# Squares of the attention output: made once a head by GpSimd and VectorE instead of tile by tile by ScalarE

## The chip, the cores and the metric

The kernel runs on one core of a Trainium2 chip. The metric is the device time of one execution in microseconds (us). The engines are TensorE (PE in the profile; PEld is its weight load), VectorE (DVE), ScalarE (ACT), GpSimd (POOL) and SyncE (SP), which issues most of the DMA transfers. SBUF is the on-chip memory of 128 partitions; PSUM is the memory into which TensorE writes its results.

## The reference, cut to what matters

Two layers of a mixer run over 512 latent and 256 context tokens. Each layer has one input projection, an RWKV-7 part, a short convolution, differential attention with 4 heads of width 128, and one output projection. The change is in the attention:

```python
def diff_attend(q, k, v, lam, scale):
    s = jnp.einsum('bqhjd,bkhjd->bhjqk', q, k).astype(jnp.float32) * scale
    p = jax.nn.softmax(s, axis=-1)
    attn = p[:, :, 0] - lam * p[:, :, 1]
    return jnp.einsum('bhqk,bkhe->bqhe', attn.astype(v.dtype), v)
...
    def finish(o, z):
        o = rms_norm(o, subln_g) * (1.0 - lam_init)
        return o.reshape(o.shape[0], o.shape[1], D_ATTN) * jax.nn.silu(z)
```

`rms_norm` divides each row of 128 outputs of a head by the root of the mean of its squares. Those sums of squares are what the change makes in another way. Layer 0 needs the outputs of all 768 tokens (6 tiles of 128 rows a head), layer 1 those of the 512 latent tokens (4 tiles).

## The kernel before, in words

The attention stage of a layer goes through the heads one by one, and through a head in units. A unit is one tile of 128 query rows, or the two context tiles together. Layer 0 has 5 units a head (`ORD`, the context unit second), layer 1 has 4. The loop at L1329 is a software pipeline written by hand: at step x, TensorE makes the scores (`sc`) of unit x+3, VectorE finds their negated row maxima (`mx`), ScalarE makes the exponentials (`e`) of unit x+2 with their sums (`oden`), VectorE makes a coefficient (`cf`) and combines the two softmaxes of unit x+1 (`e<-e,cf,e`; GpSimd does the last 256 columns, L1233 and L1234), and for unit x TensorE transposes the result (`aTp`), ScalarE copies it to SBUF (`aT`, L1257) and TensorE multiplies it with the values (`av`).

`drain` follows one unit later. ScalarE copies each 128x128 output tile of `av` from PSUM to the head's tile `O` (L1276) and runs a Square over the same PSUM tile whose accumulator gives the sum of squares in a column of `ss` (L1279, written to a scratch tile `osq`; the profile calls `ss` `oss`).

`finish` works on a whole head after its last unit, in two parts. The first part, begun one unit into the next head (`FI` = 1), loads the head's gate `zT` by a DMA from SP's queue, turns the sums into scales `ors` (a chain of some 12 small operations on VectorE: `oss`, `rs_i`, `rs_y`, `rs_t`, `ors`), and lets GpSimd scale `O` (L1297; VectorE for the last head). The second part stands behind the `av` of the next head's unit 3 (`FI2` = 3): TensorE transposes `O` (`oT`), VectorE multiplies by the gate (`zT<-oT,zT`), ScalarE casts the result (L1310) and GpSimd makes the rest to it (L1311). This place, where the finished head meets the pipeline of the next, is called a joint below; a layer has three, as the last head is finished after the stage. The place where a head's last `O` tile has been copied and the next head goes on is called a boundary.

What sets the order: TensorE's instructions keep the order of the program throughout the stage (`AL` = 1), so a transpose `oT` that waits holds up the `aTp` and the scores behind it. On VectorE and ScalarE the instructions of the unit pipeline (`dv`, `ac`) keep their order among themselves; what `finish` issues is put among them by a scheduler when the kernel is built. The PSUM tiles `aTp`, `av` and `oT` share two buffers (tag "a"). `zT` has one buffer (`ZB` = 1), so the `zT` of a head is free when L1311 of the head before has read it.

Of the kernel before, what the change touches and what calls it, by code (L numbers as in the profile page):

```python
# [10 lines left out]
F32 = mybir.dt.float32  # L11
# [3 lines left out]
ALU = mybir.AluOpType  # L15
AX = mybir.AxisListType
PSUM = bass.MemoryType.PSUM

P = 128
# [87 lines left out]
def build(tc, A):  # L107
    nc = tc.nc
    ctx = ExitStack()
    S, G = nc.scalar, nc.gpsimd  # L110
# [14 lines left out]
    V = Vec()  # L125
# [63 lines left out]
    def small(n, tag, pool=None, bufs=2):  # L189
        return (pool or sm).tile([P, n], F32, tag=tag, bufs=bufs, name=tag)  # L190
# [5 lines left out]
    for l in range(L):  # L196
        t = cst.tile([P, NCC], F32, name=f"chan{l}")
# [962 lines left out]
    def attention(l, lat, cx, pool, az_done, hd0):  # L1160
        last = l == L - 1
        li = 0.8 - 0.6 * math.exp(-0.3 * l)
        n = NL if last else NT
# [7 lines left out]
        ntt = 4 if last else 6  # L1171
        vA = pool.tile([P, 6, 512], F32, name="vA")
        ss = small(24, "oss", pool, 1)
# [11 lines left out]
        def dv(i):  # L1185
            order("v", i)

        def ac(i):
            order("s", i)
# [81 lines left out]
        def drain(u):  # L1271
            for po, tt in zip(u["po"], u["tt"]):
                if AC & 4:
                    dv(V.tensor_copy(Os[u["h"]][:, tt], po))
                else:
                    ac(S.copy(Os[u["h"]][:, tt], po))  # L1276
                osq = pool.tile([P, P], F32, tag="osq", bufs=2, name="osq")
                col = u["h"] * 6 + tt
                ac(S.activation(osq, po, AF.Square, accum_out=ss[:, col:col + 1]))  # L1279

# [1 line left out]

        def finish(h, O):
            zT = pool.tile([P, NT], F32, tag="zT", bufs=ZB, name="zT")
            nc.sync.dma_start(out=zT[:, :n], in_=zd[l][h, :, :n])
            E1 = V if h == 3 else G
            c0 = h * 6
# [3 lines left out]
            for _ in range(2):  # L1291
# [6 lines left out]
                             in1=rs[:, :ntt].unsqueeze(2).to_broadcast([P, ntt, P]), op=ALU.mult)  # L1298
# [27 lines left out]
        def at(i):  # L1326
            return us[i] if 0 <= i < len(us) else None

        for x in range(-3, len(us)):  # L1329
            u, p, c, e, w = at(x), at(x - 1), at(x + 1), at(x + 2), at(x + 3)  # L1330
# [9 lines left out]
            if p:  # L1340
                drain(p)
# [27 lines left out]
            if u and u["i"] == FI and u["h"]:  # L1369
                fins.append(finish(u["h"] - 1, Os[u["h"] - 1]))  # L1370
                next(fins[-1])
            if u and u["i"] == FI2 and u["h"]:
                next(fins[-1])
        drain(us[-1])
        fin = finish(3, Os[3])
        next(fin)
        return fin
# [75 lines left out]
    for l in range(L):  # L1453
        F.update(FL[l])
        last = l == L - 1
        n = NL if last else NT
# [248 lines left out]
```

## Time and profile before

| what | value |
|---|---|
| median of three runs | 1156.28 us (1147.5 to 1362.1) |
| the profiled execution | 1150.33 us, span 1148.3 us, mean granted clock 0.973 |
| busy share of the span | PE 90%, DVE 64%, ACT 46%, POOL 42% |
| chain that ended last, by engine | PE 36%, DVE 24%, ACT 6%, issue 6%, POOL 4%, DMA 3% |
| the gate's load into `zT`, issue to landing | 3.0 us (384 KB, layer 0), 3.1 us (256 KB, layer 1) |
| attention of layer 0, of layer 1 | some 481 to 572 us, 1008 to 1092 us of the span |

The span is the time from the profile's first instruction to its last; the execution's own time is 2.0 us longer. Shares of the whole span mix stages with different limits, so the change has to be read in the two attention stages alone.

### The profile page before, as it was taken

How to read it: one execution, taken by the hardware profiler on the slowest of the kernel's cores; microseconds unless marked ns; L12 is line 12 of the kernel's file. 1: busy time of each engine (PE TensorE's matmuls, PEld its weight loads, DVE VectorE, ACT ScalarE, POOL GpSimd, SP SyncE). 2: the span in 40 equal slices, each digit the busy share in tenths (PEclk: the TensorE clock that was granted, in tenths of full speed). 3: DMA queues.
4: the chain of work that ended last, by engine and by line, in shares of the span. 5: the costliest groups of instructions: out<-in, count | busy, mean ns of one | idle time of the engine just before them, and what ended most of it. 6: DMA issues, size and time to landing. Idle time of an engine off the chain costs nothing.

```text
span 1148.3 us, 25449 instructions
## 1 busy us (share of the span) xinstructions
PE 1034.9 (90%) x9850; PEld 847.2 (74%) x9850; DVE 731.3 (64%) x1712; ACT 523.7 (46%) x1330; POOL 488.0 (42%) x508
## 2 busy tenths in 40 slices
PE   4899989999798999989899899998987999888897
PEld 1577968777687877878787786866766897777775
DVE  3530658687666253499847857676986824579944
ACT  4332462452362232378723564654343533338731
POOL 1311534434625422464522346254474454456632
PEclk9899999999899999999999999999998999999999
DMA  9573322212423365754052452232232345555143
GB/s 350 182 245 121 89 73 57 61 31 87 141 73 112 121 189 175 223 165 108 15 188 74 147 167 88 71 100 78 72 97 85 92 132 150 165 158 170 47 156 110
DMA packets 92088, 142.55 MB, mean 124 GB/s; under 512 B 28192, under 2 KB 36416, under 8 KB 91968
## 3 DMA queue, kind: packets, MB, share of 16 engines
q1 hardware_dynamic: 88512, 136.14, 38.4%
q10 hardware_dynamic: 3456, 4.80, 1.3%
q8 instruction: 77, 1.26, 0.5%
q14 instruction: 43, 0.35, 0.1%
HBM read 110.99 MB, written 25.71 MB: 119 GB/s over the span
## 4 chain that ended last, share of the span: by engine, by line
PE 36%; DVE 24%; ACT 6%; issue 6%; POOL 4%; DMA 3%; SPq 1%; DVEq 0%; ACTq 0%; POOLq 0%
PE pcl L134 10%; PE op L134 6%; PE ptl L134 4%; DVE mx L118 4%; PE pcc L134 2%; PE ptc L134 2%; PE ch L132 2%; DVE e L118 2%; DVE bk L118 2%; DVE rs_t L118 1%; DMA mraw<-in_mod_w_dram 1%; DVE qkr L118 1%; POOL wlo L261 1%; PE av L134 1%; PE yps L132 1%
## 5 line engine op out<-in xcount | busy, mean ns | idle before, releaser
L261 POOL TENSOR_TENSOR wlo<-wraw,whi 128x512 fp32r<-128x512 f32 x134 | 181.9, 1360 | 312.2 <-ACT whi L258 279.4
L134 PE MATMUL pcl<-lat,whi 128*128 128x512 f32 (+1 forms) x928 | 295.3, 395 | 1.0 <-POOL lat L344 0.8
L134 PEld LDWEIGHTS pcl<-lat,whi 128*128 128x128 f32 x928 | 170.2, 190 | 40.2 <-issue 6.4
L134 PE MATMUL pcl<-lat,wlo 128*128 128x512 f32 (+1 forms) x464 | 185.1, 399 | 5.1 <-POOL wlo L261 3.7
L258 ACT CAST whi<-wraw 128x512 fp32r<-128x512 f32 x144 | 88.4, 618 | 159.8 <-DMA wraw<-in_w_in_dram 38.5
L134 PE MATMUL pcc<-ctx,whi 128*128 128x256 f32 x576 | 112.8, 292 | 2.0 <-DVE ctx L118 1.7
L134 PEld LDWEIGHTS pcl<-lat,wlo 128*128 128x128 f32 x464 | 88.0, 190 | 28.2 <-POOL wlo L261 5.6
L134 PEld LDWEIGHTS pcc<-ctx,whi 128*128 128x128 f32 x576 | 95.2, 197 | 9.0 <-issue 3.2
L134 PE MATMUL pcc<-ctx,wlo 128*128 128x256 f32 x288 | 84.4, 293 | 2.0 <-DVE wlo L118 2.0
L134 PE MATMUL ptl<-whi,lat 128*128 128x256 f32 x384 | 82.0, 299 | 1.1 <-ACT qkr L1090 1.1
L1222 ACT ACTIVATE e<-sc,mx 128x768 f32<-128x768 f32 (+1 forms) x80 | 66.5, 834 | 19.5 <-DVE mx L118 14.0
L118 DVE TENSOR_REDUCE mx<-sc 128x1 f32<-128x768 f32 (+1 forms) x72 | 63.7, 918 | 14.0 <-PE sc L134 14.0
L134 PE MATMUL av<-vA,aT 128*128 128x128 f32 x416 | 59.6, 287 | 14.0 <-ACT aT L1257 13.8
L134 PEld LDWEIGHTS av<-vA,aT 128*128 128x128 f32 x416 | 54.2, 195 | 20.9 <-ACT aT L1257 17.9
L134 PEld LDWEIGHTS ptl<-whi,lat 128*128 128x128 f32 x384 | 65.4, 201 | 3.4 <-ACT qkr L1090 1.4
L118 DVE TENSOR_TENSOR R<-s,cs 128x384 f32<-128x384 f32 (+1 forms) x96 | 47.0, 529 | 20.9 <-PE s L132 20.2
L134 PEld LDWEIGHTS pcc<-ctx,wlo 128*128 128x128 f32 x288 | 56.7, 197 | 4.6 <-DVE wlo L118 2.2
L134 PE MATMUL ptl<-wlo,lat 128*128 128x256 f32 x192 | 57.6, 300 | 0.0
L920 POOL TENSOR_TENSOR pz<-zu,pc 64x128 f32<-64x128 f32 x88 | 37.4, 425 | 45.9 <-DVE zu L118 41.1
L134 PE MATMUL sc<-KH,QS 128*128 128x256 f32 (+1 forms) x144 | 51.4, 371 | 4.7 <-ACT e L1222 2.9
L134 PE MATMUL sc<-KL,QS 128*128 128x256 f32 (+1 forms) x144 | 45.0, 334 | 0.0
L1233 POOL TENSOR_TENSOR e<-e,cf 128x256 f32<-128x256 f32 x32 | 26.3, 823 | 42.0 <-DVE cf L118 13.9
(449 smaller groups left out, 2450.6 us busy)
## 6 DMA issues: line engine op xcount, KB each, us to landing
wraw<-in_w_in_dram SPq DMA_DIRECT2D x144, 256.0 KB, 2.7
mraw<-in_mod_w_dram SPq DMA_DIRECT2D x96, 256.0 KB, 4.6
KH<-qd SPq DMA_DIRECT2D x32, 192.0 KB, 4.1
oraw<-in_w_out_dram SPq DMA_DIRECT2D x20, 256.0 KB, 3.7
qd<-qks SPq DMA_DIRECT2D x12, 384.0 KB, 2.4
qd<-qkr SPq DMA_DIRECT2D x12, 384.0 KB, 2.5
qks<-qkr SPq DMA_DIRECT2D x64, 64.0 KB, 2.1
zu<-vd SPq DMA_DIRECT2D x96, 32.0 KB, 2.2
```

The lines of the kernel that those rows point to most:

```text
L118: i = f(*a, **k)
L132: tc.keep_in_program_order(nc.tensor.matmul(*a, **k))
L134: i = nc.tensor.matmul(*a, **k)
L258: S.copy(hi, raw)
L261: eng.tensor_tensor(out=lo, in0=raw, in1=hi.bitcast(F32), op=ALU.subtract)
L920: G.tensor_tensor(out=pz[d][hr], in0=zu[d][hr, :, h, :], in1=prepd[d][1][hr, :, cc[d][1]].unsqueeze(2).to_broadcast([64, 2, HD]), op=ALU.mult)
L1222: ac(S.activation(ej[:, c], pb[:, c], AF.Exp, bias=mx[:, i:i + 1], accum_out=den[:, u["h"] * 6 + tt, j:j + 1]))
L1233: G.tensor_tensor(out=e1, in0=e1, in1=cf[:, 0:1].to_broadcast([P, NC]), op=ALU.mult)
```

## The change

For the first three heads of each layer `drain` only copies `O`. The sums of squares of such a head are made in `finish`: GpSimd multiplies the whole `O` tile by itself (128x768 in layer 0, 128x512 in layer 1) into the head's `zT` tile, VectorE sums each 128 columns into the head's columns of `ss`, and the load of the gate into `zT` follows. Head 3 keeps its Squares on ScalarE. `osq` has one buffer instead of two. In the changed file the square is at L1289, the reduction at L1290, the load at L1291, and the lines from the old L1285 on stand 6 further (L1297 becomes L1303, L1311 becomes L1317).

```diff
--- before.py
+++ after.py
@@ -1274,7 +1274,9 @@
                     dv(V.tensor_copy(Os[u["h"]][:, tt], po))
                 else:
                     ac(S.copy(Os[u["h"]][:, tt], po))
-                osq = pool.tile([P, P], F32, tag="osq", bufs=2, name="osq")
+                if u["h"] < 3:
+                    continue
+                osq = pool.tile([P, P], F32, tag="osq", bufs=1, name="osq")
                 col = u["h"] * 6 + tt
                 ac(S.activation(osq, po, AF.Square, accum_out=ss[:, col:col + 1]))
 
@@ -1282,6 +1284,10 @@
 
         def finish(h, O):
             zT = pool.tile([P, NT], F32, tag="zT", bufs=ZB, name="zT")
+            if h < 3:
+                sq = zT[:, :n].rearrange("p (t c) -> p t c", c=P)
+                G.tensor_tensor(out=sq, in0=O[:, :ntt], in1=O[:, :ntt], op=ALU.mult)
+                V.tensor_reduce(out=ss[:, h * 6:h * 6 + ntt], in_=sq, axis=AX.X, op=ALU.add)
             nc.sync.dma_start(out=zT[:, :n], in_=zd[l][h, :, :n])
             E1 = V if h == 3 else G
             c0 = h * 6
```

TensorE's order is the same in both kernels. On VectorE and GpSimd the order changes at every boundary and joint of the two stages.

At the boundary behind the second head of layer 0, VectorE's instructions stand in this order before (`oss`, `rs_i`, `rs_y`, `rs_t` are the finished head's chain, the rest is the unit pipeline):

```order
L118 RECIPROCAL cf<-oden 128x2
L118 SCALAR_TENSOR_TENSOR cf<-cf,lm_579,oden 128x2
L118 TENSOR_TENSOR oss<-oss,r_6473 128x6
L118 SCALAR_TENSOR_TENSOR e_6363<-e_6377,cf,e_6363 128x256 x2
L118 TENSOR_TENSOR oss<-oss,r_6473 128x6
L118 TENSOR_SCALAR oss<-oss 128x6
L118 TENSOR_SCALAR rs_i<-oss 128x6
L118 TENSOR_SCALAR rs_y<-rs_i 128x6
L118 TENSOR_TENSOR rs_t<-rs_y 128x6
L118 TENSOR_REDUCE mx<-sc 128x1 x2
```

The run of small operations ahead of `mx` is what moves in the next fence, which shows the same place in the changed kernel:

```order
L118 SCALAR_TENSOR_TENSOR cf<-cf,lm_579,oden 128x2
L118 SCALAR_TENSOR_TENSOR e_6343<-e_6357,cf,e_6343 128x256 x2
L118 TENSOR_REDUCE oss<-zT 128x6
L118 TENSOR_REDUCE mx<-sc 128x1 x2
L118 RECIPROCAL cf<-oden 128x1
L118 TENSOR_TENSOR oss<-oss,r_6451 128x6
```

The reduction now stands ahead of `mx`, and the chain behind it is spread over the units that follow.

At the first joint of layer 0, GpSimd's instructions stand in this order before:

```order
L1297 TENSOR_TENSOR O<-O,ors 128x768
L1233 TENSOR_TENSOR e_6256<-e_6256,cf 128x256
L1234 TENSOR_TENSOR e_6243<-e_6243,e_6256 128x256
L1233 TENSOR_TENSOR e_6318<-e_6318,cf 128x256
L1234 TENSOR_TENSOR e_6285<-e_6285,e_6318 128x256
L1311 TENSOR_TENSOR lat_113<-zT,lat_112 128x512
L1311 TENSOR_TENSOR ctx_115<-zT,ctx_114 128x256
```

The scaling of `O` stands two units' products ahead of L1311 there. In the changed kernel the same place reads:

```order
L1233 TENSOR_TENSOR e_6240<-e_6240,cf 128x256
L1234 TENSOR_TENSOR e_6227<-e_6227,e_6240 128x256
L1233 TENSOR_TENSOR e_6300<-e_6300,cf 128x256
L1303 TENSOR_TENSOR O<-O,ors 128x768
L1234 TENSOR_TENSOR e_6267<-e_6267,e_6300 128x256
L1317 TENSOR_TENSOR lat_113<-zT,lat_112 128x512
L1317 TENSOR_TENSOR ctx_115<-zT,ctx_114 128x256
L1289 TENSOR_TENSOR zT<-O 128x768
```

The scaling has moved back behind the `e<-e,cf` of two more units, the second of them the joint's own; the next head's square follows L1317.

VectorE's part of this joint in the changed kernel, where `rs_t` and `ors` are the last links of the finished head's chain:

```order
L118 TENSOR_REDUCE mx<-sc 128x2
L118 SCALAR_TENSOR_TENSOR rs_t<-rs_t,oss 128x6
L118 RECIPROCAL cf<-oden 128x1
L118 SCALAR_TENSOR_TENSOR ors<-rs_t,rs_y 128x6
L118 SCALAR_TENSOR_TENSOR cf<-cf,lm_579,oden 128x1
L118 TENSOR_TENSOR ors<-ors,r_6184 128x6
L118 SCALAR_TENSOR_TENSOR e_6267<-e_6300,cf,e_6267 128x512
L118 TENSOR_TENSOR zT<-oT,zT 128x384 x2
L118 TENSOR_REDUCE mx<-sc 128x1 x2
```

Before, the two `ors` stood one unit earlier, ahead of the `mx` of 128x2 that begins this fence. At the first and second joint of layer 1 the order is of the same kind; there the next head's reduction `oss<-zT` stands between the two `zT<-oT,zT` and the `mx` that follows, and its square on GpSimd stands behind L1317.

## Rows read from the trace of the kernel before

**Rows 1.** Windows, both attention stages: busy us by engine, granted clock, DMA share, GB/s.

```profile
481.00:572.00 91.00, 78.92 (x544) 70.04 (x542) 83.32 (x179) 67.78 (x214) 52.10 (x53) 0.98 0.38 112
1008.00:1092.00 84.00, 69.94 (x465) 61.36 (x463) 76.54 (x151) 56.78 (x154) 49.96 (x50) 0.98 0.40 121
```

**Rows 2.** Chain of waits, layer 0's attention: its shares, one squaring piece.

```profile
by line: DVE mx L118 25.3%; DVE e L118 11.2%; PE av L134 7.6%; ACT e L1222 7.5%; issue 5.9%; DVE rs_t L118 4.9%; DVE qkr L118 4.3%; POOL qks L1096 3.8%; ACT aT L1257 3.1%; PE aTp L142 3.1%; PE sc L134 3.1%; DVE cf L118 2.4%; DVE lat L118 2.
...
531.88 0.28 ACT osq L1279 x2
```

**Rows 3.** ScalarE's timeline in layer 0: start, duration, operation, idle before.

```profile
516.41 0.28 ACT L1279 ACTIVATE osq<-av 128x128 f32<-128x128 f32 x1
516.67 0.48 ACT L1257 COPY aT<-aTp 128x384 f32<-128x384 f32 x1
```

**Rows 4.** Who waited for the tile osq in the whole span.

```profile
...
  PEld aTp L142: 4.1, 8
...
  PEld oT L142: 3.2, 5
```

**Rows 5.** GpSimd by line and shape: busy us, mean ns, idle before.

```profile
L1233 POOL TENSOR_TENSOR e<-e,cf 128x256 f32<-128x256 f32 x32 | 26.3, 823 | 42.0 <-DVE cf L118 13.9 <-DVE rs_y L118 13.3 <-DVE rs_t L118 9.7
...
L1311 POOL TENSOR_TENSOR lat<-zT,lat 128x512 fp32r<-128x512 f32 x6 | 7.7, 1284 | 8.7 <-ACT lat L1310 8.7
...
L1297 POOL TENSOR_TENSOR O<-O,ors 128x768 f32<-128x768 f32 x3 | 4.4, 1471 | 2.6 <-DVE ors L118 2.3 <-DVE cf L118 0.3
...
L1297 POOL TENSOR_TENSOR O<-O,ors 128x512 f32<-128x512 f32 x3 | 3.1, 1041 | 1.9 <-DVE cf L118 1.5 <-DVE ors L118 0.3
```

**Rows 6.** VectorE by line and shape: reductions of squares from SBUF.

```profile
L118 DVE TENSOR_REDUCE var<-gnsq 128x16 f32<-128x1024 f32 x2 | 2.4, 1220 | 1.9 <-ACT gnsq L1000 1.9
...
L118 DVE TENSOR_REDUCE var<-gnsq 128x8 f32<-128x512 f32 x1 | 0.7, 679 | 0.0
```

**Rows 7.** Timeline of GpSimd and VectorE at the third joint of layer 0.

```profile
567.95 1.47 POOL L1297 TENSOR_TENSOR O<-O,ors 128x768 f32<-128x768 f32 x1 [0.30 <-DVE cf L118]
...
567.97 1.46 DVE L118 SCALAR_TENSOR_TENSOR cf<-cf,lm,oden 128x1 f32<-128x1 f32 x1
```

**Rows 8.** VectorE's timeline, from layer 0's first joint to the next head.

```profile
530.31 1.28 DVE L118 TENSOR_REDUCE mx<-sc 128x2 f32<-128x512 f32 x2
...
531.69 0.22 DVE L118 SCALAR_TENSOR_TENSOR cf<-cf,lm,oden 128x1 f32<-128x1 f32 x1
...
534.85 1.82 DVE L118 TENSOR_REDUCE mx<-sc 128x1 f32<-128x768 f32 x2 [0.48 <-PE sc L134]
...
537.43 0.88 DVE L118 SCALAR_TENSOR_TENSOR e<-e,cf,e 128x256 f32<-128x256 f32 x2
538.23 0.16 DVE L118 TENSOR_TENSOR oss<-oss,r 128x6 f32<-128x6 f32 x1
...
539.12 1.81 DVE L118 TENSOR_REDUCE mx<-sc 128x1 f32<-128x768 f32 x2
```

**Rows 9.** TensorE's timeline at the first joint of layer 0 and of layer 1.

```profile
532.20 0.55 PE L142 MATMUL oT<-ident,O 128*128 128x128 f32 x3 [0.58 <-ACT osq L1279]
532.58 0.49 PE L142 MATMUL aTp<-ident,e 128*128 128x128 f32 x3
...
1059.52 0.66 PE L142 MATMUL oT<-ident,O 128*128 128x128 f32 x4 [1.25 <-POOL O L1297]
```

**Rows 10.** VectorE's timeline, layer 1: first joint, then the end of the stage.

```profile
1058.27 1.81 DVE L118 TENSOR_REDUCE mx<-sc 128x1 f32<-128x768 f32 x2
...
1065.27 1.81 DVE L118 TENSOR_REDUCE mx<-sc 128x1 f32<-128x768 f32 x2
...
1089.14 1.02 DVE L118 SCALAR_TENSOR_TENSOR cf<-cf,lm,oden 128x1 f32<-128x1 f32 x1
```

**Rows 11.** Windows of 2 us: a gap in TensorE's work, and behind it.

```profile
509.00:511.00 2.00, 1.05 (x6) 0.86 (x6) 1.97 (x6) 2.00 (x5) 0.31 (x1) 0.84 0.88 316
511.00:513.00 2.00, 2.00 (x10) 1.90 (x9) 1.93 (x6) 1.05 (x7) 1.54 (x2) 0.50 1.01 310
```

## The prediction

> **What bounds the kernel now.** TensorE is busy nine tenths of the span, but the change touches only the two attention stages, so I read those first. In their windows [rows 1] VectorE is busy 83.3 of 91.0 us and 76.5 of 84.0, TensorE 78.9 and 69.9, ScalarE 67.8 and 56.8, GpSimd 52.1 and 50.0. The reader should see that VectorE leaves only 7.7 + 7.5 = 15.2 us, and that ScalarE, which the change relieves, has the most slack but GpSimd. The chain of waits says the same [rows 2]: the maxima `mx` and the combination `e` on VectorE have 36.5% of layer 0's stage. The squaring on ScalarE is in that chain for heads 0 to 2 only in four pieces of 0.28 us (one is shown), all in layer 0, at two joints and two boundaries; in layer 1 none of these heads is. So the stage turns on VectorE's order and on the hand-overs at joints and boundaries, and I read the timelines there.
>
> **What it takes from ScalarE.** Thirty Squares go: 3 heads of 6 tiles and 3 of 4. A Square starts at 516.41 and the copy of `aT` behind it at 516.67 [rows 3], so each holds 0.26 us of ScalarE, 7.8 us in all. Little of it is on the path. Two bounds: 4 x 0.28 = 1.1 us by the chain, and 4.1 + 3.2 = 7.3 us by the time for which the transposes `aTp` and `oT` waited for an `osq` to free the shared PSUM buffer [rows 4]. The second counts waits of head 3 too, which stays, and delays behind which VectorE was late anyway. I take 1.1, since the chain is what leads to the end.
>
> **What it adds.** GpSimd gets three squares of 128x768 and three of 128x512. Its scaling of `O` in the same shapes, from the same tile, takes 1.47 and 1.04 us [rows 5], so 3 x 1.47 + 3 x 1.04 = 7.5 us; the scaling also has two inputs. VectorE gets six reductions. Reducing 512 squares takes 0.68 us, 1024 take 1.22 [rows 6]; 768 lie half way, 0.95. That is 3 x 0.95 + 3 x 0.68 = 4.9 us on the engine that has 15.2 us left.
>
> **Boundaries of layer 0 (three).** Before, the products `e` end at 537.43 + 0.88 = 538.31, small operations of the `ors` chain fill the time from 538.23 to 539.12, and `mx` starts [rows 8]. After, the reduction stands ahead of that `mx` and waits for the square, which waits for the head's last copy of `O`. If the square ran fully beside `e`, the reduction would add its 0.95, and the 0.89 of small operations, which move on into later units, would leave about +0.5 (with the hand-overs between engines). If square and `e` exclude each other, it is 1.47 + 0.95 - 0.89 = +1.5. The nearest row speaks for the second: beside GpSimd's scaling of `O`, 567.95 to 569.42, a `cf` of VectorE that started 0.02 later took 1.46 us [rows 7], against 0.22 elsewhere [rows 8]. If the moved small operations cost again in full, it is 2.4. I take 1.5 each, 4.5 us, with 0.5 to 2.4 each as ends.
>
> The Trainium skill, page "SBUF — State Buffer", section "Who interferes with whom", says that a VectorE operation with two SBUF inputs and a GpSimd operation that reads SBUF shut each other out for a whole instruction, and that `tensor_reduce` on this chip never does so. The row on `cf` agrees with the first half; no row shows a reduction from SBUF beside GpSimd. Were squares and reductions free of each other and of everything else, as the second half alone would have it, the boundaries would cost 3 x 0.5 = 1.5 us in place of 4.5.
>
> **Joints of layer 0.** This is the largest term. Before, `ors` is ready a unit early, GpSimd scales `O` ahead of the joint, and the `oT` behind `av` wait at most a little: the second waits 0.58 us, for an `osq` [rows 9]. After, the chain starts later, because the sums come at once from a reduction after the boundary and not tile by tile, and VectorE's order has one small operation of it between two large ones. Its last link now stands behind the joint's `mx`, and the scaling on GpSimd behind the joint's `e<-e,cf`. Count from the end of that `mx`, T = 530.31 + 1.28 = 531.6 [rows 8]. Five small operations take some 0.55 (six take 0.89, above); the product by `cf` on GpSimd ends at some T + 1.1 (0.62 alone, 0.82 on average [rows 5]); the scaling takes 1.47, so with two hand-overs `O` is ready at T + 2.7 to T + 3.0. Then two groups of `oT` and VectorE's product, which frees the PSUM buffer, lead to `aTp` at about T + 4.0. Before, `aTp` starts at 532.58, T + 1.0 [rows 9]. So +3.0 us, with everything behind it on TensorE: `aTp`, the scores, and the `mx` of 534.85, which already waits for the scores [rows 8]. Twice (first and second joint) 6.0. At the third the scaling already stands as late [rows 7], so nothing. Lower end 0, if waits elsewhere take it up; upper end 3.3 each.
>
> **Layer 1.** At its first joint TensorE already waits 1.25 us for the scaled `O` [rows 9]. New is that the next head's square must wait for L1317, the last reader of the single `zT`, and that VectorE's queue has the reduction between the products `zT` and the next `mx`. Behind `zT` come L1317 at 1.28, the square at 1.04 and the reduction at 0.68 [rows 5, 6], 3.0 us in which `mx` is shut out. VectorE had other work there: its `mx` stand at 1058.27 and 1065.27 [rows 10], and the `cf` and `e` between them now come ahead. I take 2.2 for each of two joints, between 0.7 (the reduction alone) and 3.0, nearer the upper end as TensorE waits for the scaling there already. The first boundary costs its reduction, 0.7. At the end of the stage a `cf` of 1.02 beside GpSimd's scaling goes ahead of it, -0.8 against 0.22 [rows 10, 8]. Sum 4.4 + 0.7 - 0.8 = 4.3.
>
> **At nothing.** The gate's load moves behind the reduction in SP's queue. The gate is read a joint later, some three units of 3 to 4 us; the loads behind it in that queue are weights and a later head's operands. If that cover were gone, it would cost up to one landing a head, 3.0 or 3.1 us by the table of the profile. One `osq` buffer is enough for the ten Squares that stay. At the start of layer 0's stage two products trade places; from -1 to +1.5, taken as 0.
>
> **Sum.** 4.5 + 6.0 + 4.3 - 1.1 = 13.7 us. Against the profiled execution of 1150.3 this is 1164.0 us. That execution lies between the lowest and the median of the three runs (1147.5 and 1156.28), so the median after may lie up to 6 us above this for the spread alone.
>
> **Rivals.**
> *The joints absorb it.* TensorE's wait at a joint is covered, as VectorE and ScalarE work off their queues meanwhile and VectorE's small operations fall into it; only boundaries and layer 1's reductions remain. Against it: the `mx` after the joint waits for scores already. 4.5 + 0.7 + 2 x 0.7 - 0.8 - 1.1 = +4.7, 1155 us.
> *Faster.* The relief is the whole 7.3 us of waits for `osq`, the reductions fall in VectorE's 15.2 us of idle time, and the boundaries cost their lower end of 0.5: -7.3 + 1.5 + 0.7 = -5.1, 1145 us. Against it: the chain shows only 1.1 us of that wait.
> *Slower by over 2%: the clock falls.* TensorE, half idle from 509 to 511 us (1.05 of 2.00 busy), was granted 0.50 of its clock in the next window, 1.2 of 2.4 GHz, and it was then busy throughout [rows 11]. If each of six joints and four boundaries makes a gap long enough, 2 us at half the clock is 1 us of lost work each time, and the reduced clock trails on before it returns; at 1.0 to 1.4 us each ten places give +10 to +14 on the forecast, 1174 to 1178. It decides where the gaps at the joints reach 2 us or more and the engine behind them is TensorE; the stages' mean clock was 0.98 [rows 1], and VectorE is the bound, which speaks against it.
> *It doesn't do what it says.* The order shows 30 Squares gone and six squares and reductions in their place, so this has no chance of its own.
>
> **How the numbers follow.** Two percent, about what a measurement of this kernel can tell from no change, is 23 us. Chances: the forecast 0.61, absorbed 0.18, faster 0.09, clock 0.12. The predicted time is the forecast's 1164. Its own ends: 1.5 + 0 + (0.7 + 1.4 - 0.8) - 7.3 = -4.5 gives 1146; 7.2 + 6.6 + (0.7 + 6.0 - 0.8) = 19.7, without relief, gives 1170; with the spread of 6 us above, 1176. The range 1147 to 1176 takes in the absorbed case and about half of the clock's, and leaves out most of the faster one. Only a part of the faster case, with runs that spread, would come out over 2% faster: 0.02. Over 2% slower is the clock and the upper tail of the forecast: 0.13. Within 2%: 0.85.
>
> **What would show it.** The profile after should show `osq` ten times; GpSimd's squares at 1.4 to 1.5 and 1.0 to 1.1 us; reductions at 0.9 to 1.0 and 0.7; `oT` at the first two joints of layer 0 with an idle time of 2 to 3 us released by GpSimd's `O`, where it was under 0.6; VectorE waiting for GpSimd ahead of its reductions; layer 0's stage longer by some 9 us and layer 1's by some 4. I am wrong if the waits at the joints are there but the stages are no longer, if the stages shorten (ScalarE was more of a limit than the chain says), or if the granted clock behind the joints drops to one half.

## The result, and the profile after

The changed kernel takes 1167.51 us (median of 6 runs), the kernel before 1153.77 us in the same comparison; the ratio is 1.0152, with a 95% interval of 1.0117 to 1.0188. One of the six runs of the kernel before, 1362.1 us, fell in a slower state and counts in that median, but not in the ratio, which compares fast runs alone. The change makes the kernel slower by 1.5%, or 17.5 us (13.5 to 21.7 by the interval), which is inside two percent and clear of noise. The profiled execution of the changed kernel took 1158.85 us.

First the page of the kernel after, busy time:

```profile
PE 1036.3 (90%) x9850; PEld 850.6 (74%) x9850; DVE 735.3 (64%) x1718; ACT 518.0 (45%) x1270; POOL 495.9 (43%) x514
```

The work is about what was forecast: ScalarE is busy 518.0 us in place of 523.7 (5.7 less, where 7.8 was forecast), VectorE 735.3 in place of 731.3 (4.0 more, forecast 4.9), GpSimd 495.9 in place of 488.0 (7.9 more, forecast 7.5). The chain of this trace breaks off after 4% of the span, in the output projection, so it can't be used here; timelines of single engines have to do.

TensorE has the same instructions in the same order in both kernels. So the length of a stage can be taken from one instruction to the same one later: from the stage's first `aTp` to the first `oT` of the last head. TensorE's timeline of the kernel before, these four places (start, duration, operation):

```profile
492.01 0.49 PE L142 MATMUL aTp<-ident,e 128*128 128x128 f32 x3
...
582.97 0.82 PE L142 MATMUL oT<-ident,O 128*128 128x128 f32 x6
...
1025.29 0.49 PE L142 MATMUL aTp<-ident,e 128*128 128x128 f32 x3
...
1103.55 0.60 PE L142 MATMUL oT<-ident,O 128*128 128x128 f32 x4
```

And the same four places after:

```profile
485.60 0.49 PE L142 MATMUL aTp<-ident,e 128*128 128x128 f32 x3
...
586.32 0.82 PE L142 MATMUL oT<-ident,O 128*128 128x128 f32 x6
...
1026.43 0.84 PE L142 MATMUL aTp<-ident,e 128*128 128x128 f32 x3
...
1112.20 0.60 PE L142 MATMUL oT<-ident,O 128*128 128x128 f32 x4
```

Layer 0's stage grows from 582.97 - 492.01 = 91.0 to 100.7 us, layer 1's from 78.3 to 85.8: +9.8 and +7.5, together 17.3, against 0.0152 x 1153.8 = 17.5 us by the ratio. In these two executions the whole cost lies in the two stages. (The two profiled executions differ by 8.5 us only: ahead of layer 0's attention this execution was 6.4 us faster than the one of before, as the first `aTp` at 485.60 and 492.01 shows, and between the stages 2.2 us, in parts that the change does not touch. One execution is not enough to judge a change of this size by its span, and that 17.3 comes so near to 17.5 is in part chance: see the table of places behind the experiments.)

The four joints that changed, in TensorE's timeline after; the bracket is the idle time before, and what ended it:

```profile
530.02 1.45 PE L142 MATMUL oT<-ident,O 128*128 128x128 f32 x6 [3.79 <-POOL O L1303]
531.49 0.90 PE L142 MATMUL aTp<-ident,e 128*128 128x128 f32 x3
...
553.35 0.91 PE L142 MATMUL oT<-ident,O 128*128 128x128 f32 x6 [2.58 <-POOL O L1303]
...
1066.78 1.11 PE L142 MATMUL oT<-ident,O 128*128 128x128 f32 x4 [4.38 <-POOL O L1303]
...
1088.02 0.66 PE L142 MATMUL oT<-ident,O 128*128 128x128 f32 x4 [2.54 <-POOL O L1303]
```

Where `oT` waited at most 0.58 us in layer 0 and 1.25 in layer 1 [rows 9], it now waits 3.79, 2.58, 4.38 and 2.54 us for GpSimd's scaling of `O`. At the first joint of each layer the scaling stands behind the joint's own `e<-e,cf`. At the second joints it stands ahead of that product and is late all the same, as GpSimd waits for `ors`, the last link of the chain:

```profile
551.83 1.47 POOL L1303 TENSOR_TENSOR O<-O,ors 128x768 f32<-128x768 f32 x1 [0.97 <-DVE ors L118]
553.25 1.06 POOL L1233 TENSOR_TENSOR e<-e,cf 128x256 f32<-128x256 f32 x1
...
1086.93 1.04 POOL L1303 TENSOR_TENSOR O<-O,ors 128x512 f32<-128x512 f32 x1 [1.36 <-DVE ors L118]
```

VectorE at the first joint and the boundary behind it:

```profile
526.26 0.68 DVE L118 TENSOR_REDUCE mx<-sc 128x2 f32<-128x512 f32 x1
...
527.45 1.19 DVE L118 SCALAR_TENSOR_TENSOR e<-e,cf,e 128x512 f32<-128x512 f32 x1
530.87 1.20 DVE L118 TENSOR_TENSOR zT<-oT,zT 128x384 f32<-128x384 f32 x2 [2.23 <-PE oT L142]
534.76 1.82 DVE L118 TENSOR_REDUCE mx<-sc 128x1 f32<-128x768 f32 x2 [2.69 <-PE sc L134]
...
536.69 1.30 DVE L118 SCALAR_TENSOR_TENSOR cf<-cf,lm,oden 128x2 f32<-128x2 f32 x1
538.09 0.88 DVE L118 SCALAR_TENSOR_TENSOR e<-e,cf,e 128x256 f32<-128x256 f32 x2
538.89 0.95 DVE L118 TENSOR_REDUCE oss<-zT 128x6 f32<-128x768 f32 x1
539.75 1.81 DVE L118 TENSOR_REDUCE mx<-sc 128x1 f32<-128x768 f32 x2
```

VectorE waits 2.23 us for `oT` ahead of `zT`, and 2.69 us for the scores ahead of `mx`, which waited 0.48 before [rows 8]. At the boundary the `cf` lasts 1.30 us, beside this square on GpSimd, and the reduction starts right behind `e` without a wait:

```profile
528.05 1.92 POOL L1303 TENSOR_TENSOR O<-O,ors 128x768 f32<-128x768 f32 x1
...
536.50 1.47 POOL L1289 TENSOR_TENSOR zT<-O 128x768 f32<-128x768 f32 x1 [0.97 <-ACT O L1276]
```

The scaling itself lasts 1.92 us here, beside VectorE's `e` of 527.45; before it took 1.47 [rows 5]. At both joints of layer 1 VectorE waits for the square, in front of its `mx`; each line of TensorE is the last of the scores made ahead of that `mx`:

```profile
1071.63 0.69 DVE L118 TENSOR_REDUCE oss<-zT 128x4 f32<-128x512 f32 x1 [3.16 <-POOL zT L1289]
1072.47 1.82 DVE L118 TENSOR_REDUCE mx<-sc 128x1 f32<-128x768 f32 x2 [0.15 <-PE sc L134]
...
1071.81 0.63 PE L134 MATMUL sc<-KL,QS 128*128 128x512 f32 x1
...
1092.52 0.69 DVE L118 TENSOR_REDUCE oss<-zT 128x4 f32<-128x512 f32 x1 [3.16 <-POOL zT L1289]
1093.12 1.81 DVE L118 TENSOR_REDUCE mx<-sc 128x1 f32<-128x768 f32 x2
...
1092.07 0.63 PE L134 MATMUL sc<-KL,QS 128*128 128x512 f32 x1
```

The wait of 3.16 us is long, but it holds up little. At the first joint the reduction ends at 1072.32 and the scores, late behind `oT`, at 1072.44: `mx` waits for the scores. At the second the scores end at 1092.70, and `mx` starts 0.4 us later, behind the reduction.

At the first boundary of layer 1 the square, on GpSimd from 1044.91 us, stands beside VectorE's `qkr`, which lasts 1.51 us, and the reduction comes ahead of `e`; the last line is the same `qkr` in the kernel before:

```profile
1044.99 1.51 DVE L118 TENSOR_TENSOR qkr<-qkr,qks 128x512 f32<-128x512 f32 x1 [0.31 <-POOL qks L1096]
...
1048.40 0.68 DVE L118 TENSOR_REDUCE oss<-zT 128x4 f32<-128x512 f32 x1
...
1048.63 0.61 POOL L1233 TENSOR_TENSOR e<-e,cf 128x256 f32<-128x256 f32 x1 [1.10 <-DVE cf L118]
...
1043.58 0.69 DVE L118 TENSOR_TENSOR qkr<-qkr,qks 128x512 f32<-128x512 f32 x1 [0.31 <-POOL qks L1096]
```

What TensorE's clock did is seen in windows around two of the joints (length; busy time of PE, PEld, DVE, ACT, POOL; granted clock; DMA share; GB/s):

```profile
526.00:530.00 4.00, 0.23 (x3) 0.04 (x1) 2.60 (x9) 0.40 (x3) 2.83 (x4) 1.00 0.48 118
530.00:533.00 3.00, 2.96 (x11) 2.42 (x12) 1.11 (x2) 0.52 (x2) 0.65 (x1) 0.53 0.00 0
...
1063.00:1067.00 4.00, 0.22 (x1) 0.22 (x2) 2.79 (x9) 0.22 (x1) 2.33 (x3) 0.88 0.00 0
1067.00:1073.00 6.00, 5.56 (x23) 4.77 (x23) 1.97 (x4) 3.37 (x8) 3.95 (x4) 0.51 0.14 46
```

TensorE was busy 0.23 of 4.00 us ahead of the first joint and ran at full clock, and behind it was busy throughout at 0.53 of its clock, close to the lower of its two levels (1.2 of 2.4 GHz). It was at 0.50 for some us behind the other joints too (554.2 to 557.4 and 1090.1 to 1093.3 us); before, it stayed at 1.00 behind the same four (531 to 537, 552 to 558, 1060 to 1066 and 1077 to 1083 us).

The prices of the added operations:

```profile
L1289 POOL TENSOR_TENSOR zT<-O 128x768 f32<-128x768 f32 x3 | 4.4, 1467 | 3.7 <-ACT O L1276 3.7
...
L1289 POOL TENSOR_TENSOR zT<-O 128x512 f32<-128x512 f32 x3 | 3.1, 1039 | 0.2
```

```profile
L118 DVE TENSOR_REDUCE oss<-zT 128x6 f32<-128x768 f32 x3 | 2.8, 946 | 0.0
...
L118 DVE TENSOR_REDUCE oss<-zT 128x4 f32<-128x512 f32 x3 | 2.0, 683 | 6.3 <-POOL zT L1289 6.3
```

Squares of 1.47 and 1.04 us and reductions of 0.95 and 0.68 us are the forecast's figures. The last column shows where a reduction had to wait: nowhere in layer 0, 6.3 us in layer 1.

### The profile page after: what moved, and what is told of

Read it like the earlier page. It is cut to its first block, busy times and chain, and to the rows that moved or that the text cites. A ratio compares the mean times of both kernels' runs of the same rounds, so it can differ in the third digit from the quotient of the medians.

```text
span 1157.0 us, 25406 instructions
## 1 busy us (share of the span) xinstructions
PE 1036.3 (90%) x9850; PEld 850.6 (74%) x9850; DVE 735.3 (64%) x1718; ACT 518.0 (45%) x1270; POOL 495.9 (43%) x514
## 5 line engine op out<-in xcount | busy, mean ns | idle before, releaser
L134 PE MATMUL pcc<-ctx,whi 128*128 128x256 f32 x576 | 110.1, 288 | 1.8 <-DVE ctx L118 1.7
L134 PE MATMUL ptl<-whi,lat 128*128 128x256 f32 x384 | 79.1, 292 | 0.0
L134 PE MATMUL sc<-KH,QS 128*128 128x256 f32 (+1 forms) x144 | 56.3, 402 | 5.4 <-ACT e L1222 2.9
L1233 POOL TENSOR_TENSOR e<-e,cf 128x256 f32<-128x256 f32 x32 | 30.9, 966 | 44.3 <-DVE cf L118 10.3
L134 PE MATMUL sc<-KL,QS 128*128 128x256 f32 (+1 forms) x144 | 49.7, 363 | 0.0
```

What stands on the lines that cost most here:

```text
L134: i = nc.tensor.matmul(*a, **k)
L1233: G.tensor_tensor(out=e1, in0=e1, in1=cf[:, 0:1].to_broadcast([P, NC]), op=ALU.mult)
```

## The experiments

The table has all kernels: the ratio to the kernel before with its interval, the mean granted clock over the timed runs, and how much longer each stage was in the profiled execution, between the same two instructions as above. The stages of one execution scatter by some us, so the ratio decides.

| kernel | ratio (95%) | clock | layer 0 | layer 1 |
|---|---|---|---|---|
| before | 1 | 0.973 | 91.0 us | 78.3 us |
| changed | 1.0152 (1.0117 to 1.0188) | 0.965 | +9.8 | +7.5 |
| 1, chain has precedence | 1.0119 (1.0083 to 1.0156) | 0.968 | +10.0 | +6.2 |
| 2, own tile for squares | 1.0109 (1.0069 to 1.0149) | 0.965 | +12.3 | +3.4 |
| 3, Squares taken away | 1.0032 (1.0002 to 1.0063) | 0.971 | +3.5 | +1.5 |
| 4, layer 0 only | 1.0086 (1.0053 to 1.0120) | 0.966 | +11.8 | +0.4 |
| 5, 1 and 2 together | 1.0125 (1.0092 to 1.0158) | 0.968 | +6.8 | +3.9 |
| 6, 5, reduction behind `mx` | 1.0175 (1.0123 to 1.0227) | 0.965 | +12.5 | +6.8 |
| 7, fillers at the joints | 1.0206 (1.0160 to 1.0251) | 0.964 | +11.7 | +8.2 |
| 8, 5, square on ScalarE | 1.0082 (1.0054 to 1.0110) | 0.971 | +7.9 | +3.8 |
| 9, late scaling alone | 1.0136 (1.0094 to 1.0178) | 0.964 | +9.0 | +6.3 |
| 10, added work alone | 1.0140 (1.0094 to 1.0187) | 0.963 | +8.1 | +2.3 |
| 11, small Squares | 1.0059 (1.0031 to 1.0086) | 0.969 | +3.9 | +2.0 |
| 12, small Squares, pinned | 1.0022 (0.9995 to 1.0049) | 0.971 | +3.8 | +2.0 |

**1. The chain has precedence.**

```diff
+            with tc.high_priority(offset=100):
                 V.reciprocal(r0[:, :ntt], d_)
                 ...
                 E1.tensor_tensor(out=O[:, :ntt], in0=O[:, :ntt], ...
```

> The changed kernel with one thing altered: the chain that turns the sums into scales has precedence over the unit pipeline when the order is made, so that at the joints the scaling of O on GpSimd stands ahead of the joint's product by cf again, and ors ahead of the joint's mx. Squares and reductions stay where they are. Theory 1 (late scaling at the joints, 10.4 of the 13.7 us forecast): the waits of oT for O (3.8, 2.6, 4.4 and 2.5 us in the changed kernel) fall under 1.5 us and the ratio to the kernel before falls from 1.015 to 1.005 to 1.009. Rival 2 (the reduction ahead of mx, and the square before it, shut mx out): the waits fall too, but the ratio stays at 1.012 or above. Rival 3 (the clock): the ratio follows the number of stretches at half the clock in the stages, whatever oT waits.

The ratio came to 1.0119, just under the 1.012 from which rival 2 begins and above theory 1's 1.009. Its interval holds both, and overlaps that of the changed kernel. The waits did fall, at the first joint of layer 0 to this (TensorE's timeline):

```profile
542.79 0.87 PE L142 MATMUL oT<-ident,O 128*128 128x128 f32 x6 [1.56 <-POOL O L1304]
```

and to 1.56 us at the second too, and to 0.28 and 0.86 us in layer 1, and the clock behind these joints stayed at 1.00 (542 to 545 and 564 to 567 us). Layer 0's stage is as long as in the changed kernel all the same, but 8.0 of its 10.0 us were lost ahead of the first joint in this execution; from the last `av` ahead of that joint on it lost 2.0 us, where the changed kernel lost 7.2. Of these 8.0 us, 6.2 went at the stage's start, where all engines have the changed kernel's order, which lost 1.7 us there: that part isn't the edit's. So the profile speaks for theory 1 at the joints, and the ratio leaves the size open. Experiment 9 was made to settle it.

**2. A tile of its own for the squares.**

```diff
-                sq = zT[:, :n].rearrange("p (t c) -> p t c", c=P)
+                sq = pool.tile([P, NT], F32, tag="sqb", bufs=1, name="sqb")[:, :n].rearrange("p (t c) -> p t c", c=P)
```

> The changed kernel with a tile of its own for the squares in place of zT, so that the gate's load need not wait for the reduction, and the next head's square need not wait for the last reader of zT. The forecast gave 2.2 us to each of two joints of layer 1 for that: if right, 2 to 5 us less in layer 1, nothing in layer 0, ratio 1.011 to 1.013. If the late scaling alone makes the cost of the joints, no change: 1.014 to 1.016.

The ratio of 1.0109 is at the lower edge of what was expected, and layer 1's stage lost 3.4 us in place of 7.5: the shared `zT` cost some 4 us there. Layer 0 did not gain. But the edit moved the late scaling too: `oT` waited 2.43 and 0.00 us in layer 1, where the changed kernel has 4.38 and 2.54. At the first joint the scheduler put the scaling ahead of the joint's product, and behind it the reduction that starts the next chain came 1.4 us after the start of `oT` in place of 4.9. So this experiment doesn't tell the square's wait from the late scaling. The intervals overlap, so the profile carries this more than the ratio.

**3. Squares taken away.**

```diff
-                osq = pool.tile([P, P], F32, tag="osq", bufs=2, name="osq")
+                if u["h"] < 3:
+                    if tt == ntt - 1:
+                        ac(S.activation(ss[:, u["h"] * 6:u["h"] * 6 + ntt], po[:, :ntt], AF.Square))
+                    continue
+                osq = pool.tile([P, P], F32, tag="osq", bufs=1, name="osq")
```

> Only what the change takes away: thirty Squares go, and nothing makes the sums; one Square of 4 or 6 columns a head stands in for them (so the normalisation is left out), which keeps the chain behind the head's last tile. By the forecast the relief of ScalarE is worth 1.1 us: ratio 0.997 to 1.001. By the rival 'faster' it is 7.3 us: 0.992 to 0.995.

Neither: with less work the kernel became a little slower, 1.0032 (12 runs). One place where it lost is in VectorE's timeline of this kernel, behind the first joint:

```profile
532.57 1.20 DVE L118 SCALAR_TENSOR_TENSOR e<-e,cf,e 128x512 f32<-128x512 f32 x1
533.69 0.69 DVE L118 TENSOR_SCALAR rs_i<-oss 128x6 int32<-128x6 int32 x1
534.42 1.19 DVE L118 TENSOR_SCALAR rs_y<-rs_i 128x6 f32<-128x6 f32 x1
535.64 0.65 DVE L118 TENSOR_TENSOR rs_t<-rs_y 128x6 f32<-128x6 f32 x1
...
536.61 1.81 DVE L118 TENSOR_REDUCE mx<-sc 128x1 f32<-128x768 f32 x2
```

Links of the chain (`rs_i`, `rs_y`, `rs_t`), which take 0.17 us alone, last 0.69, 1.19 and 0.65 us here, back to back with GpSimd's operations, and stand ahead of `mx`, which starts 4.0 us after `e`; before it was 2.55 us, from 532.30 to 534.85. With the Squares gone the scheduler placed the chain elsewhere, and here in a worse place. These 1.5 us are a part of the 5.0 that the two stages lost; another 1.6 went at the start of layer 0's stage, where VectorE and GpSimd have the order of before. That the new order is the cause of the whole isn't shown.

**4. The change in layer 0 alone.**

```diff
-                if u["h"] < 3:
+                if u["h"] < 3 and l == 0:
                     continue
...
-            if h < 3:
+            if h < 3 and l == 0:
                 sq = zT[:, :n].rearrange("p (t c) -> p t c", c=P)
```

> The change in layer 0 alone; layer 1 as before. By the forecast's terms 4.5 + 6.0 - 1.1 = 9.4 of 13.7 us: ratio 1.007 to 1.010. If layer 1 costs more than its 4.3 us, as the profile after suggests, the measured 1.015 is split about evenly: 1.007 to 1.008 here. If the cost is the clock's, it need not split so.

1.0086 is 9.9 us of 1150 (6.1 to 13.8 by the interval), which agrees with the forecast's 9.4 for layer 0. Layer 1 is left with 17.5 - 9.9 = 7.6, but two intervals of about 4 us each way stand behind that difference, so it doesn't exclude the forecast's 4.3.

The trace gives more. In layer 0 every engine has the changed kernel's order here, and `oT` waits the same 3.80 and 2.58 us, but the clock stayed low for longer behind these waits. Windows of 10 us over the first joint, the changed kernel and then this one:

```profile
529.00:539.00 10.00, 8.96 (x56) 8.12 (x57) 5.21 (x9) 6.30 (x19) 5.09 (x5) 0.83 0.00 1
...
536.10:546.10 10.00, 8.98 (x46) 8.05 (x47) 4.27 (x7) 5.16 (x17) 4.85 (x5) 0.66 0.00 0
```

Mean clocks of 0.83 and 0.66 are 3.4 and 6.8 us at half clock. Counted to the next head, the two joints cost 4.5 and 3.8 us here, 3.2 and 2.8 in the changed kernel. So 3.4 us more at half clock went with 1.0 to 1.3 us, with the same waits.

**5. Both edits together** (the diffs of 1 and 2).

> Both edits of the first two experiments at once: the chain has precedence, and the squares have a tile of their own. Alone they took 3.3 and 4.3 thousandths off the changed kernel's 1.0152. If the joints of layer 0 (late scaling) and the joints of layer 1 (square behind the last reader of zT, reduction ahead of mx) are two separate costs, they add: ratio 1.006 to 1.009. If both took away the same wait, it stays near 1.011.

1.0125: the two did not add, and the miss shows how loosely waits and time go together here. `oT` waits 1.91, 1.57, 0.27 and at most 0.3 us, yet behind the first two the clock fell again, to 0.58 and 0.56 over 3 us.

**6. The reduction behind `mx`** (on top of 5).

```diff
-FI = 1
+FI = 0
...
-                V.tensor_reduce(out=ss[:, h * 6:h * 6 + ntt], in_=sq, axis=AX.X, op=ALU.add)
+                dv(V.tensor_reduce(out=ss[:, h * 6:h * 6 + ntt], in_=sq, axis=AX.X, op=ALU.add))
```

> The kernel with both edits, and the reduction placed behind the boundary's mx in VectorE's order, so that the square on GpSimd runs beside mx and nothing of VectorE's pipeline waits for it. The boundaries are then left with the reductions' own time. Theory (boundaries 1.5 us each in layer 0, of which the wait is about 0.5 to 1): 2 to 4 us less than with both edits alone, ratio 1.003 to 1.006. If VectorE is full and only its added 4.9 us of reductions count, no change: 1.006 to 1.009.

Worse than both answers: 1.0175. VectorE doesn't wait for the square at the boundary, but everything behind the reduction comes later, and `oT` waits 2.38, 2.37, 3.54 and 2.04 us. What a later start of the chain costs at the joints is more than what the boundary gives back.

**7. Fillers at the joints.**

```diff
+                for _ in range(14 if t0 == 0 and h < 3 else 0):
+                    T.transpose(pt[:, :P], ident, ident)
                 for tt in range(t0, t1):
                     T.transpose(pt[:, (tt - t0) * P:(tt - t0 + 1) * P], O[:, tt], ident)
```

> The changed kernel with 14 transposes of the identity put on TensorE ahead of each oT group of heads 0 to 2 (about 1.7 us at full clock, into the same PSUM tile, overwritten by oT), so that TensorE is busy for part of the wait for O. Theory 1 (the wait itself is the cost): the fillers are free and useless, ratio 1.013 to 1.017. Rival 3 (the clock that falls behind the wait costs): mean clock of the runs up from 0.9645 towards 0.970, ratio 1.008 to 1.012.

1.0206, slower than the changed kernel by its point value, with the clock at 0.964 as there. The real `oT` still waited 2.27, 1.06, 2.86 and 1.00 us behind the fillers, and the clock fell behind the two longer ones. Behind the two shorter ones, at the second joints, it stayed at 1.00: these joints lost 2.0 and 0.1 us, where the changed kernel lost 2.8 and 0.6 with a clock of one half, though fillers and wait together kept `oT` 0.2 us longer. At layer 0's third joint, where `oT` had nothing to wait for, the fillers cost some 1.0 us of their own. Over the runs they did not raise the clock, so the ratio doesn't measure its price.

**8. The square on ScalarE, once a head** (on top of 5).

```diff
-                G.tensor_tensor(out=sq, in0=O[:, :ntt], in1=O[:, :ntt], op=ALU.mult)
+                S.activation(sq, O[:, :ntt], AF.Square)
```

> The kernel with both edits, but the square of a head made by one ScalarE operation over the whole O tile (about 0.9 us by the exponential of 768 columns) in place of GpSimd's 1.47. If the price of a boundary is the square's time and its exclusion with VectorE, 2 to 4 us less than with both edits: ratio 1.003 to 1.006; if it is the reduction on VectorE, no change; if ScalarE's slack is the limit, more: over 1.009.

1.0082: 4.3 thousandths, some 5 us, less than with GpSimd's square, and the best of the kernels that make the sums once a head. ScalarE takes 0.85 and 0.63 us for the two shapes. By the point values GpSimd's square is a cost of its own, but not the larger one; the intervals overlap, and in the two profiles the stages don't show it (11.7 us lost in place of 10.7).

**9. The late scaling alone**, in the kernel before:

```diff
+            if h < 3:
+                last_e["sc"] = G.tensor_tensor(out=O[:, :ntt], in0=O[:, :ntt], ...).ins
...
+                if "sc" in last_e:
+                    tc.add_manual_dep(last_e.pop("sc"), em.ins.name, ...)
```

> The kernel before, with all its Squares on ScalarE, and one thing altered: at the joints GpSimd's scaling of O stands behind the joint's product by cf, where the changed kernel has it. TensorE's order is unchanged, and no square or reduction is added. The forecast priced this at 3.0 us for each of two joints of layer 0; with 1 to 2 us for each of two in layer 1 that is 8 to 10 us: ratio 1.006 to 1.009. The small gain of the precedence of the chain (3 thousandths of the ratio at most) says 2 to 4 us: 1.002 to 1.004. If it costs nothing, below 1.001, the joints are no cause.

1.0136, more than was expected: this move, with no square and no reduction added and no Square taken away, costs nearly what the whole change costs. (The scheduler's order on VectorE moved along with it: in layer 0 the joint's `e` now stands ahead of both products `zT`.) TensorE's timeline at its joints:

```profile
536.26 1.54 PE L142 MATMUL oT<-ident,O 128*128 128x128 f32 x6 [3.04 <-POOL O L1307]
...
560.39 1.54 PE L142 MATMUL oT<-ident,O 128*128 128x128 f32 x6 [3.04 <-POOL O L1307]
...
1074.83 0.66 PE L142 MATMUL oT<-ident,O 128*128 128x128 f32 x4 [4.39 <-POOL O L1307]
...
1097.25 1.11 PE L142 MATMUL oT<-ident,O 128*128 128x128 f32 x4 [4.31 <-POOL O L1307]
```

Waits as long as the changed kernel's are all there. The edit puts the scaling behind the joint's product at every joint, so at the second joints, where the changed kernel has it ahead, they are longer: 3.04 in place of 2.58 and 4.31 in place of 2.54 us. So this kernel shows what late scaling costs, and more of it than the change makes. The clock falls behind the waits (windows as above):

```profile
533.00:536.00 3.00, 0.21 (x2) 0.02 (x1) 2.85 (x5) 1.06 (x6) 2.51 (x3) 1.00 0.02 8
536.00:539.00 3.00, 2.73 (x11) 2.24 (x12) 1.87 (x3) 0.20 (x1) 1.33 (x2) 0.51 0.29 87
```

Layer 0 lost 9.0 us, layer 1 6.3.

**10. The added work alone**, in the kernel before, with its Squares kept:

```diff
+            if h < 3:
+                sq = pool.tile([P, NT], F32, tag="sqb", bufs=1, name="sqb")[:, :n].rearrange("p (t c) -> p t c", c=P)
+                G.tensor_tensor(out=sq, in0=O[:, :ntt], in1=O[:, :ntt], op=ALU.mult)
+                V.tensor_reduce(out=small(6, "s2", pool)[:, :ntt], in_=sq, axis=AX.X, op=ALU.add)
```

> The kernel before, its Squares kept and used, with GpSimd's six squares and VectorE's six reductions added beside them into tiles that nothing reads. So no chain waits for them; they only take their places on the two engines. The forecast's terms for that are the boundaries (4.5 us), and the reductions of layer 1 (2.1 us): ratio 1.005 to 1.007. If VectorE's idle time takes them up, 1.000 to 1.002.

1.0140, but it does not isolate what it should: the reductions pushed the chain back here too, and GpSimd's scaling with it. In layer 0 `oT` waits 2.30 and 2.38 us for `O`. The two joints took 7.3 of the 10.4 us that its profile lost. So added work that nothing reads is paid at the joints as well.

**11 and 12. Small Squares.** In 11 the Squares of heads 0 to 2 are narrow; in 12 VectorE's order at two joints is pinned as well.

```diff
-                ac(S.activation(osq, po, AF.Square, accum_out=ss[:, col:col + 1]))
+                qn = 8 if u["h"] < 3 else P
+                ac(S.activation(osq[:, :qn], po[:, :qn], AF.Square, accum_out=ss[:, col:col + 1]))
```

```diff
+            if pins:
+                after(pins[0], ci.ins)
...
+                if pins:
+                    after(si.ins, pins[0])
+                    after(pins[1], si.ins)
+                    pins.clear()
```

> The kernel before with the Squares of heads 0 to 2 over 8 columns in place of 128 (so the normalisation of these heads uses a part of the sum), which leaves the order of VectorE and GpSimd nearly as it was and takes some of ScalarE's time away, at most 0.12 us of the 0.26 each. If the relief of ScalarE is worth what the forecast says, the ratio is 0.998 to 1.001, and the 1.003 of the kernel without Squares came from its other order; if less work for ScalarE costs time for another reason, such as the clock, it is 1.002 or more.

> The kernel with small Squares, and at the first two joints of layer 0 the order of VectorE that the kernel before has: the first product zT, then the joint's e, then the second zT (the kernel with small Squares has e ahead of both or behind both, and its aTp waited 1.8 us for zT). If its 1.0059 came from that order, the two joints give back 2.8 and 1.1 us of layer 0 and the ratio falls to 1.000 to 1.003. If it stays at 1.004 or above, the lighter ScalarE costs time for another reason.

1.0059 and 1.0022; the intervals touch, and the stages of the two profiles are equally long, so that the pin mended it isn't shown. In both the loss starts at layer 0's first joint (2.6 us in 11, 2.5 us in 12), where VectorE has a weight's `wo21lo` ahead of the joint that stood behind it before, and `aTp` waits for `zT`, which it didn't before [rows 9]; of 12:

```profile
532.24 0.55 PE L142 MATMUL aTp<-ident,e 128*128 128x128 f32 x3 [1.85 <-DVE zT L118]
```

What both show is that a lighter ScalarE made no kernel faster.

## Why the prediction was right

**The time and the sign.** 1164 us was forecast and 1167.5 measured; 13.7 us more was forecast and 17.5 measured by the ratio. Theory 1, the late scaling at the joints, is the largest cost, as forecast: experiment 9 makes it with no work added or taken away, and experiment 1 takes most of it back in its profile. The other terms agree with the forecast less well than the sum does.

**Where the time went.** The table gives, for the profiled executions, how many us later than in the kernel before TensorE starts the same `av`, counted from the stage's first `aTp` and split by places. In layer 0 a place ends at the first `av` of a head or at the one ahead of a joint: 518.13, 528.08, 538.66, 548.99, 558.89 and 568.74 us before, 513.43, 524.18, 537.96, 548.73, 561.39 and 571.72 in the changed kernel. In layer 1 the head behind a joint wins some of it back, so there a joint counts up to the `av` ahead of the next: 1056.77, 1075.26 and 1092.76 before, 1060.81, 1083.28 and 1101.34 changed. The forecast's relief of 1.1 us has no place of its own.

| place | forecast | changed | 1 | 2 | 9 |
|---|---|---|---|---|---|
| layer 0, up to the second head | 0 | 1.7 | 6.2 | 4.6 | 1.4 |
| its three boundaries | 4.5 | 1.7 | 2.6 | 1.6 | 0.1 |
| its first joint | 3.0 | 3.2 | 0.3 | 2.7 | 3.7 |
| its second joint | 3.0 | 2.8 | 1.0 | 2.9 | 3.8 |
| from the third joint on | 0 | 0.4 | -0.1 | 0.4 | 0.0 |
| layer 1, up to the first joint | 0.7 | 2.9 | 3.5 | 1.4 | 0.0 |
| its first joint | 2.2 | 4.0 | 1.4 | 1.2 | 4.0 |
| its second joint | 2.2 | 0.6 | 1.2 | 0.7 | 2.2 |
| the rest | -0.8 | 0.1 | 0.1 | 0.1 | 0.1 |

The first row can't be put down to the change: experiment 9 has there the order of the kernel before on every engine and lost 1.4 us, experiment 1 the order of the changed kernel and lost 6.2 in place of 1.7. The four joints are 10.5 of the 17.3 us in the changed kernel, 4.0 in experiment 1 and 13.7 in experiment 9.

**Joints of layer 0** were the largest term and were priced at 3.0 us each; they cost 3.2 and 2.8. At the first joint the steps can be followed: T, the end of the `mx`, is 526.26 + 0.68 = 526.94; `oT` starts at 530.02, T + 3.1, where T + 2.7 to T + 3.0 was forecast. The next `aTp` came at 531.49, T + 4.55, against T + 1.0 before, so +3.5 in place of +3.0. At the first `av` behind it the first joint had cost 3.8 us, the second 3.4, of which a unit later 0.6 were won back. The excess goes with two things that the sum left out: the scaling lasts 1.92 us beside `e`, and TensorE goes on at half its clock. (The five small operations were put at 0.55 us, although the row's 0.89 for six would give 0.74; they took 0.51.) At the second joint the forecast has the size, but not the path: the scaling isn't behind the joint's product there, but waits for `ors`.

**Layer 1** was under-priced, 4.3 against 7.5, and not where it seemed. Its joints cost 4.6 us in all where 4.4 was forecast, but that agreement is luck. The forecast had `mx` shut out by the reduction behind the square; the reduction waits 3.16 us at both joints, but `mx` had to wait for its scores at the first, and lost at most 0.4 us at the second. What the joints cost is again the late `oT`, with waits of 4.38 and 2.54 us. The shared `zT` has its part in that, as the next head's chain starts later behind it (experiment 2). What was missing in the sum is the first boundary, 2.9 us up to the joint in place of 0.7: the square stands beside `qkr`, which lasts 0.8 us longer, the reduction adds its 0.68, and the clock was at 0.50 from 1049.0 to 1052.4 us. The gain of 0.8 at the stage's end was not seen either.

**Boundaries of layer 0** were over-priced at 1.5 each: TensorE lost 0.8, 0.4 and 0.5 us, near the forecast's lower end. The exclusion is seen, a `cf` of 1.30 us beside the square, against 0.22, but the reduction took the place of the small operations: from the start of `e` to `mx` it is 539.75 - 538.09 = 1.66 us after and 539.12 - 537.43 = 1.69 before [rows 8]. What is left on VectorE is the longer `cf`, and only a part of its 1.1 us reached TensorE. The Trainium skill, page "SBUF — State Buffer", section "Who interferes with whom", has VectorE's operations with two SBUF inputs shut out by GpSimd's that read SBUF. The `cf` agrees with it, and so does the scaling that grew from 1.47 to 1.92 us.

**The relief** of 1.1 us was not found. Experiments 3, 11 and 12 took ScalarE's work away and came out at 1.003, 1.006 and 1.002; none is below 1. Intervals of about 3 us each way, and orders that moved along, leave 1.1 us open; the 7.3 us of waits for `osq` [rows 4] did not come back as time.

**The rival of the clock** had a chance of 0.12, and the prediction named a clock of one half behind the joints as a sign that it was wrong. That sign came true, as a part of the forecast's own mechanism: at all four late joints the clock fell to one half, and the mean over the timed runs fell from 0.973 to 0.965. The forecast had counted on VectorE as the bound; at the joints it was TensorE that others waited for. Twice (1 - clock) times the time is the time at half clock: 63 us before, 83 after. Within the runs of single kernels (166 runs of 14 kernels) a run with 1 us more of it is 0.39 us longer, so 20 us go with 7.7 of the mean difference of 15.6. That is a correlation. Experiments 4 and 7 have joints of the changed kernel's order with more and with less time at half clock: in layer 0 3.4 us of it went with 0.7 to 1.3 us a joint, of the 2.8 to 3.2 that a late joint costs there. These are single executions; so the wait seems the larger part, and the share over all runs stays open.

**The other rivals.** That the joints absorb their waits (1155 us) and that the kernel gets faster (1145 us) are refuted.

**What stays open.** The ratios do not add: the late scaling alone costs 1.0136, the added work alone 1.0140, both with the rest 1.0152, and giving the chain precedence took about a fifth off by the point values. The profiles show why in part: the late scaling alone is later than in the change, the added work makes the scaling late too, and precedence at the joints was paid for with 1.5 us more at the boundaries. That the sum came out within 4 us owes much to errors of both signs: boundaries of layer 0 at 4.5 for 1.7, the first boundary of layer 1 at 0.7 for 2.9, a relief and a gain that were not there.

## What to carry to other kernels

In a software pipeline whose engine order is fixed, price a change by when its result reaches the place where another stream must take it, not by the busy time it moves: here a scaling that stood a few places later in GpSimd's queue at four joints cost 1.4%, with no work added. Before work is moved off an engine, look whether that engine's work is late anywhere; taking the Squares from ScalarE gained nothing. And where a scheduler places small dependent operations, an edit elsewhere can move them in front of a large one, so compare the built orders at the hand-overs before pricing anything.

## What the runs showed of the hardware

Small VectorE operations on a handful of columns, 0.17 us each alone, lasted 0.65 to 1.30 us when they fell together with a GpSimd operation on SBUF tiles (experiment 3, and the `cf` at 536.69). A reduction from SBUF did not: at 1048.40 it lasted 0.68 us beside GpSimd's `e<-e,cf` of 0.61, each as long as alone. A wait of TensorE of 2.5 to 4.4 us was followed, at all four late joints of the changed kernel and of experiment 9, by a stretch at about half the granted clock; in experiment 5 this also followed waits of 1.9 and 1.6 us, while in experiment 1 it did not follow two of 1.56 us. Such stretches stand elsewhere in the stages too, in other places from one execution to the next (from 502.9 to 506.2 us in the changed kernel, from 510.4 to 513.7 us in the kernel before).
